# Activations stored features-first, their two parts side by side, and passes of 320, 256 and 288 columns in one product

## The chip, the cores and the metric

The kernel runs on one core of a Trainium2 chip. The metric is the device time of one execution in microseconds (us); the median of three runs is compared. TensorE (PE) does matrix products, VectorE (DVE) and ScalarE (ACT) elementwise work, GpSimd (POOL) some of it, and SyncE (SP) issues most transfers.

## What is computed

One layer of a hybrid decoder for 288 tokens (a prompt of 256 and 8 samples of 4), model width 2048, float32:

```python
h = rms_norm(x, g_pre)
z = h @ w_in                        # q | k | v | u | v_g
A = block-sparse attention over q, k, v (samples also read a paged cache of 2048 past tokens)
B = gelu(u) * (tril(w_spatial) @ layer_norm(gelu(v_g)) + b_spatial)
mix = (sigmoid(h @ wg_a) * (A @ w_a_out) + sigmoid(h @ wg_b) * (B @ w_b_out)) @ w_o
x = x + rms_norm(mix, g_post_mix)
a1, g1 = split(rms_norm(x, g_pre_ffn) @ w_ffn_in)          # 2 x 5632 columns
x = x + rms_norm((silu(a1) * g1) @ w_ffn_out, g_post_ffn)
x = x + (p @ w_ple) * sigmoid(rms_norm(x, g_ple) @ w_ple_gate)
```

It returns x (called y), the new k and v rows for the cache and the normalised v_g rows of the samples.

## The kernel before, in words

**Layout.** Every activation lies in SBUF with 128 features on the partitions and the 288 tokens (T) along the row, one such block for each of 16 feature groups k (KD = 16). In memory x, p, y and the k rows have tokens first, so the kernel turns them on TensorE with transposes of 128x128: x at the start (`turn` in `h_parts`, L147, tile `pt`), x once more for the residual while w_o runs (tile `xc`), p (tile `ptok`), the spatial weights (L469, `wt`), the k rows on their way out (`to_tokens`, L315, `tt`) and y at the end (L1045, `yt`).

**Product.** All weight products go through `product` (L236 to 260): 256 output columns of a weight at a time, as two halves t of 128, each with an accumulator of 288 float32 in a PSUM bank. Every float32 factor is split into a high and a low part of the type fp32r. A weight tile `wr` of 512 KB (four k) is loaded by SP (L245), ACT casts it to `wh` (L248), DVE subtracts to get `wl` (L249). For each k and t three passes of 288 columns follow: wh with the activation's high part (L255), wh with its low part (L256), wl with the high part (L257). A tile thus feeds 24 passes. There are 496 tiles of four k and 24 of two, which makes 4064 triples or 12,192 passes. Four buffers hold `wr`, three each `wh` and `wl`.

**Stages.** In order of time: q (tiles `hh`, `hl` from x), k, v, v_g, the gates and u with b between them while the cache is read and the sample scores and values are computed (to 699 us), a (w_a_out, to 750), o (w_o, to 857), the norm and residual, fa and fg (w_ffn_in, first half, 869 to 1151), f (w_ffn_out, first half, 1152 to 1293), fa and fg again (1300 to 1572), f again (to 1713.7), norm and residual, pg (w_ple_gate, 1726.6 to 1835), and the tail that adds up y and stores it. `le` is the small product with w_ple that is put into the two norms. f has 16 accumulators over 22 k each in two halves, so 704 triples; when one is complete, `fo_done` copies or adds it to `fo` (L1008, L1010).

**Order.** The instruction order of each engine comes from a scheduler; every engine works its queue in that order. At the start SP's queue interleaves parts of x, the weight tiles of w_in and pages of the key cache (`kt`).

Of the kernel before, what the change touches and what calls it, by code (L numbers as in the profile page):

```python
# [10 lines left out]
F32 = mybir.dt.float32  # L11
# [97 lines left out]
def tile_hybrid_step(ctx: ExitStack, tc: tile.TileContext, a: dict, o: list):  # L109
    nc = tc.nc  # L110
    y_p, y_s, kp_o, vp_o, ks_o, vs_o, gv_o = o
# [20 lines left out]

    cst = perm.tile([128, 128], F32, name="cst")
    nc.sync.dma_start(cst, a["c_perm"][:, :128])
# [7 lines left out]
    TP = 3 * 128  # L142

    def turn(pt, tiles, c):

        for j, t in enumerate(tiles):
            nc.tensor.transpose(pt[:, j * 128:j * 128 + 128], t[:, c], ident)  # L147

    xp = a["x_prompt"].rearrange("b s d -> (b s) d")
    xs = a["x_sample"].rearrange("b s d -> (b s) d")  # L150
    srcs = [(xp[0:128], 128), (xp[128:256], 128), (xs, TS)]
    XC = 512
    x_tok = [[p_x0.tile([128, XC], F32, name=f"x{j}_{c}") for j in range(3)] for c in range(D // XC)]

    def x_load(c):
        for (src, n), t in zip(srcs, x_tok[c]):
            nc.sync.dma_start(t[:n], src[:, c * XC:c * XC + XC])

    for tiles in x_tok:
        clear_rows(tiles[2])  # L160
    x_load(0)
    names = ["g_pre_mix", "g_post_mix", "g_pre_ffn", "g_post_ffn", "g_ple", "g_vnorm"]
    glist = [a[name].rearrange("l (k p) -> (l k) p", p=128) for name in names]
    gl0 = p_x0.tile([16, 128], F32, name="gl0")
    nc.scalar.dma_start(gl0, glist[0])
    gl = p_x0.tile([72, 128], F32, name="gl")
    for i, g in enumerate(glist[1:]):
        nc.gpsimd.dma_start(gl[16 * i:16 * i + g.shape[0]], g)
# [19 lines left out]
    def turned_gains(gl, n):  # L188
        gains = perm.tile([128, n], F32, name=f"gains{n}")
        gp = bank([128, n], "gp")  # L190
        nc.tensor.transpose(gp, gl, ident[:n, :n])
        nc.vector.tensor_copy(gains, gp)
        return gains

    g_pre = turned_gains(gl0, 16)

# [9 lines left out]
    hh = p_h.tile([128, KD, T], F32R, name="hh")  # L206
    hl = p_h.tile([128, KD, T], F32R, name="hl")

    def h_parts(c):
        for i in range(XC // 128):  # L210
            k = c * (XC // 128) + i
# [4 lines left out]
            nc.vector.scalar_tensor_tensor(hl[:, k], pt, g_pre[:, k:k + 1], hh[:, k], op0=ALU.mult, op1=ALU.subtract)  # L216

    def square_sums(c):
        for j in range(3):
            junk = p_x0.tile([128, XC], F32, name="junk", bufs=2)  # L220
            nc.scalar.activation(junk, x_tok[c][j], AF.Square, accum_out=sums[:, j, c:c + 1])

    sums = p_x0.tile([128, 3, D // XC], F32, name="sums")
    r0 = p_h.tile([128, T], F32, name="r0")

    def r0_of():
        st = p_x0.tile([128, 3], F32, name="st")
        nc.vector.tensor_reduce(st, sums, axis=AX.X, op=ALU.add)
        r0p = bank([128, TP], "r0p")
        for j in range(3):  # L230
            dg = p_x0.tile([128, 128], F32, name="dg", bufs=3)
            nc.vector.tensor_scalar(dg, ident, st[:, j:j + 1], None, op0=ALU.mult)
            nc.tensor.matmul(r0p[:, j * 128:j * 128 + 128], ones_d, dg, start=True, stop=True)
        rstd_of(r0, r0p[:, :T], p_x0.tile([128, T], F32, name="r0t"))


    def product(w, c0, ks, part, done, name, of="acc"):
# [26 lines left out]
    def hpart(k):  # L264
        return hh[:, k], hl[:, k]
# [9 lines left out]
    for c in range(D // XC):  # L275
        h_parts(c)
        for q in q2:
            next(q)
        if c + 1 < D // XC:
            x_load(c + 1)  # L280
        square_sums(c)
    r0_of()
    gains = turned_gains(gl, 72)
    g_pm, g_pf, g_pof, g_pl, g_vn = (gains[:, 16 * i:min(16 * i + 16, 72)] for i in range(5))
# [146 lines left out]
    def gmlp_gen():  # L431
# [26 lines left out]
        def prep_gen():  # L458
            gm = p_g.tile([128, C_GM], F32, name="gm")
            nc.sync.dma_start(gm, a["c_gm"])  # L460
            wsp = p_g.tile([128, H, 128], F32, name="wsp", tag="vn")
            nc.sync.dma_start(wsp, a["w_spatial"].rearrange("l g t s -> t (l g) s"))
            nc.sync.dma_start(brow, a["b_spatial"].rearrange("l g t -> l (g t)").to_broadcast([128, H * 128])
                              .rearrange("p (g t) -> p g t", t=128))
            tri = gm[:, C_TRI:C_TRI + 128][:, None, :].to_broadcast([128, 4, 128])
            for g in range(0, H, 4):
                tp = bank([128, 4, 128], "wt")
                for t in range(4):
                    nc.tensor.transpose(tp[:, t], wsp[:, g + t], ident)  # L469
                nc.vector.tensor_tensor(wst[:, g:g + 4], tp, tri, ALU.mult)  # L470
                yield 0.5
# [40 lines left out]
        def done_u(x, h):  # L512
            vn = late["vn"]
            for t in range(2):
# [24 lines left out]
    def gate_gen():  # L539
# [25 lines left out]
        for g in range(8):  # L565
            yield from product(w_b, g * GC, K8, lambda k: (bb[:, 0, k], bb[:, 1, k]), lambda x, g=g: done_b(x, g), "b")
# [257 lines left out]
    ah = p_ab.tile([128, H, T], F32R, name="ah")  # L824
    al = p_ab.tile([128, H, T], F32R, name="al")
# [6 lines left out]
    mh = p_m.tile([128, KD, T], F32R, name="mh")  # L832
    ml = p_m.tile([128, KD, T], F32R, name="ml")
# [3 lines left out]
    def mix_gen():  # L837
        for g in range(8):
# [8 lines left out]
            yield from product(w_a, g * GC, K8, lambda k: (ah[:, k], al[:, k]), done, "a")  # L847
# [6 lines left out]

    p_xt, end_xt = pool("p_xt", "left")
    for c in range(4):
        xc = [p_xt.tile([128, 512], F32, name=f"xc{j}", bufs=2) for j in range(3)]
        clear_rows(xc[2])
        for (src, n), t in zip(srcs, xc):
            nc.sync.dma_start(t[:n], src[:, c * 512:c * 512 + 512])  # L860
        for k in range(4):
            pt = bank([128, TP], "pt")
            turn(pt, xc, slice(k * 128, k * 128 + 128))
            nc.vector.tensor_copy(x1[:, 4 * c + k], pt[:, :T])
# [41 lines left out]
    for g in range(8):  # L906
        drain(product(w_o, g * GC, K16, lambda k: (mh[:, k], ml[:, k]), lambda x, g=g: wo_done(x, g), "o"))

    p_z, end_z = pool("p_z", "right")
    zh = p_z.tile([128, KD, T], F32R, name="zh")  # L910
    zl = p_z.tile([128, KD, T], F32R, name="zl")
# [21 lines left out]
    pp_ = a["p_prompt"].rearrange("l b s c -> (l b s) c")  # L933
    ps_ = a["p_sample"].rearrange("l b s c -> (l b s) c")
    psrc = [(pp_[0:128], 128), (pp_[128:256], 128), (ps_, TS)]
    p_tok = [p_n.tile([128, PLE], F32, name=f"ptok{j}", tag="yt", bufs=3) for j in range(3)]
    clear_rows(p_tok[2])
    for (src, n), t in zip(psrc, p_tok):
        nc.sync.dma_start(t[:n], src)
    ph = p_n.tile([128, 2, T], F32R, name="ph")  # L940
    pl = p_n.tile([128, 2, T], F32R, name="pl")
    for k in range(2):
        pt = bank([128, TP], "pt")
        turn(pt, p_tok, slice(k * 128, k * 128 + 128))
        pt = pt[:, :T]
        nc.scalar.copy(ph[:, k], pt)
        nc.vector.tensor_tensor(pl[:, k], pt, ph[:, k], ALU.subtract)
# [27 lines left out]
    def zpart(k):  # L975
        return zh[:, k], zl[:, k]
# [111 lines left out]
```

## Time and profile before

| | |
|---|---|
| median of three runs | 1848.33 us (1846.85 to 1848.41) |
| the profiled execution: its time | 1845.0 us |
| its span, first to last instruction | 1843.2 us |
| PE busy | 1822.8 us, 99% |
| DVE, ACT, POOL busy | 52%, 42%, 5% |
| mean granted TensorE clock | 0.997 |
| moved by DMA | 414.83 MB, mean 225 GB/s |

The duration of a PE row contains its way through a pipeline: passes that begin 133 ns apart show some 296 ns each. What a pass costs in a full stream is therefore read from the distance of the starts (the chain in order of time, or the count of passes in a window), not from its mean duration.

### The profile page before, as it was taken

Reading aid. Unit: us, or ns where it says so; the run is one execution under the profiler, and the core shown is the slowest. Engines: PE = TensorE matmul, PEld = TensorE weight load, DVE = VectorE, ACT = ScalarE, POOL = GpSimd, SP = SyncE. Lnnn points to the kernel's source line nnn. Section 1 sums busy time; section 2 is a strip of 40 time slices with the busy share of each in tenths; the row PEclk is TensorE's granted clock in tenths of the full one; section 3 lists DMA queues with packets and bytes.
Section 4 is the critical chain, followed back from the end, with each engine's and each line's share of the span. In section 5 each row is a group of like instructions: output and inputs, shape, how many; then the busy total and the mean of one; then the engine's idle time right before and its main releaser. Section 6 shows DMA issues by size and latency. Waiting matters only on the chain.

```text
span 1843.2 us, 38883 instructions
## 1 busy us (share of the span) xinstructions
PE 1822.8 (99%) x16004; PEld 1775.4 (96%) x16004; DVE 951.8 (52%) x1357; ACT 775.2 (42%) x1090; POOL 97.8 (5%) x195
## 2 busy tenths in 40 slices
PE   8999999999999999999999999999999999999898
PEld 8999899999999989999999999999999999999898
DVE  4754446544444347635855554433545545444764
ACT  5334455434333344445533333333333333434643
POOL 2010112000000000110000000000000000001000
PEclk9999999999999999999999999999999999999999
DMA  9589999999999985544555554445555555444452
GB/s 344 168 297 350 329 354 329 365 344 363 356 340 353 374 280 180 181 164 138 167 162 170 162 170 162 163 163 166 172 162 170 162 170 162 164 161 155 137 192 101
DMA packets 312673, 414.83 MB, mean 225 GB/s; under 512 B 13544, under 2 KB 275296, under 8 KB 312496
## 3 DMA queue, kind: packets, MB, share of 16 engines
q1 hardware_dynamic: 311120, 409.23, 64.7%
q8 instruction: 125, 2.05, 0.4%
q0 software_dynamic: 1200, 2.76, 0.4%
q10 hardware_dynamic: 176, 0.37, 0.1%
q14 instruction: 52, 0.43, 0.1%
HBM read 407.45 MB, written 4.85 MB: 224 GB/s over the span
## 4 chain that ended last, share of the span: by engine, by line
PE 97%; DVE 1%; ACT 1%; issue 0%; DMA 0%; SPq 0%; DVEq 0%
PE f L256 5%; PE f L257 5%; PE fa L257 5%; PE f L255 5%; PE fg L257 5%; PE fg L255 5%; PE fg L256 5%; PE fa L255 5%; PE fa L256 5%; PE values L732 3%; PE scores L634 3%; PE ga L255 2%; PE pg L255 2%; PE gb L255 2%; PE ga L256 2%; PE pg L257 2%
## 5 line engine op out<-in xcount | busy, mean ns | idle before, releaser
L249 DVE TENSOR_TENSOR wl<-wr,wh 128x1024 fp32r<-128x1024 f32 (+1 forms) x520 | 623.9, 1201 | 719.9 <-ACT wh L248 708.1
L248 ACT CAST wh<-wr 128x1024 fp32r<-128x1024 f32 (+1 forms) x520 | 535.8, 1031 | 896.0 <-PE f L256 165.2
L257 PE MATMUL f<-dh,wl 128*128 128x288 f32 x704 | 208.9, 297 | 0.0
L256 PE MATMUL f<-dl,wh 128*128 128x288 f32 x704 | 208.5, 296 | 0.0
L255 PE MATMUL f<-dh,wh 128*128 128x288 f32 x704 | 207.5, 295 | 0.0
L255 PE MATMUL fg<-zh,wh 128*128 128x288 f32 x704 | 207.3, 295 | 0.0
L257 PE MATMUL fg<-zh,wl 128*128 128x288 f32 x704 | 207.2, 295 | 0.0
L257 PE MATMUL fa<-zh,wl 128*128 128x288 f32 x704 | 206.7, 295 | 0.5 <-DVE wl L249 0.5
L256 PE MATMUL fa<-zl,wh 128*128 128x288 f32 x704 | 206.0, 294 | 0.9 <-DVE zl L925 0.9
L256 PE MATMUL fg<-zl,wh 128*128 128x288 f32 x704 | 206.9, 294 | 0.0
L255 PE MATMUL fa<-zh,wh 128*128 128x288 f32 x704 | 204.7, 295 | 1.0 <-ACT zh L924 1.0
L256 PEld LDWEIGHTS fa<-zl,wh 128*128 128x128 f32 x704 | 132.5, 188 | 1.2 <-DVE zl L925 1.2
L257 PEld LDWEIGHTS fa<-zh,wl 128*128 128x128 f32 x704 | 132.0, 188 | 0.7 <-DVE wl L249 0.7
L256 PEld LDWEIGHTS fg<-zl,wh 128*128 128x128 f32 x704 | 132.7, 188 | 0.1
L256 PEld LDWEIGHTS f<-dl,wh 128*128 128x128 f32 x704 | 132.6, 188 | 0.0
L255 PEld LDWEIGHTS fa<-zh,wh 128*128 128x128 f32 x704 | 131.4, 188 | 1.2 <-ACT zh L924 1.2
L255 PEld LDWEIGHTS f<-dh,wh 128*128 128x128 f32 x704 | 132.3, 188 | 0.1
L255 PEld LDWEIGHTS fg<-zh,wh 128*128 128x128 f32 x704 | 132.3, 188 | 0.0
L257 PEld LDWEIGHTS fg<-zh,wl 128*128 128x128 f32 x704 | 132.1, 188 | 0.1
L257 PEld LDWEIGHTS f<-dh,wl 128*128 128x128 f32 x704 | 132.1, 188 | 0.1
L255 PE MATMUL pg<-zh,wh 128*128 128x288 f32 x256 | 76.1, 304 | 5.4 <-ACT zh L924 5.4
L255 PE MATMUL gb<-hh,wh 128*128 128x288 f32 x256 | 76.7, 299 | 0.0
(356 smaller groups left out, 3792.2 us busy)
## 6 DMA issues: line engine op xcount, KB each, us to landing
wr<-in_w_ffn_in SPq DMA_DIRECT2D x176, 512.0 KB, 3.4
kt<-in_cache_k SPq DMA_DIRECT2D x128, 512.0 KB, 7.4
vt<-in_cache_v SPq DMA_DIRECT2D x128, 512.0 KB, 6.5
wr<-in_w_in SPq DMA_DIRECT2D x80, 512.0 KB, 6.3
wr<-in_w_ffn_out SPq DMA_DIRECT2D x80, 512.0 KB, 3.2
wr<-in_w_gate SPq DMA_DIRECT2D x64, 512.0 KB, 6.8
wr<-in_w_o SPq DMA_DIRECT2D x32, 512.0 KB, 3.2
wr<-in_w_ple_gate SPq DMA_DIRECT2D x32, 512.0 KB, 3.2
```

The costliest lines, as they stand in the source:

```text
L248: nc.scalar.copy(wh[:, :m], raw[:, :m])
L249: nc.vector.tensor_tensor(wl[:, :m], raw[:, :m], wh[:, :m], ALU.subtract)
L255: nc.tensor.matmul(accs[t], wh[:, i, c], xh, start=k == 0, stop=False)
L256: nc.tensor.matmul(accs[t], wh[:, i, c], xl, start=False, stop=False)
L257: late["mm"] = nc.tensor.matmul(accs[t], wl[:, i, c], xh, start=False, stop=k == n - 1)
L634: i = nc.tensor.matmul(sp[b][32 * g:32 * g + 32, 4 * n:4 * n + 4], Q[:, h2, g, dq], kt[:, :, c:c + 32], start=h2 == 1 and dq == 0, stop=h2 ...
L732: i = nc.tensor.matmul(oa[b][32 * g:32 * g + 8], w[:, n, 32 * g + 8 * part:32 * g + 8 * part + 8], v[:, :, g], start=first and part == 3, ...
```

## The change

The host hands over x, p, the gains and w_spatial with features on the partitions, and takes y and the k rows in that form, so all transposes of these are gone; k and y are stored straight from the tiles `kT` and `x1`. x comes in four pieces of 590 KB (`xs`), and for the residual once more in one transfer of 2.36 MB into `x1`. The mean of the squares at the start is taken from squares of `xs` (ACT, in place), DVE additions and two float32 matmuls over 288 columns, instead of row sums and three matmuls over 128. The high and low parts of an activation lie side by side in one tile (`hhl`, `ahl`, `mhl`, `phl`, `zhl`, `dhl`, `bb`), a row of 2x288. With that, `product` has a parameter `wide`: the first pass takes 288 + wide columns, so that it also does the first `wide` columns of wh times low; the second pass does the remaining 288 - wide; the third is as before. The first columns of the low part land in extra columns of the accumulator, which ACT copies out (`rest`) and DVE adds. `wide=32` is given to f alone (320, 256, 288); elsewhere it is 0.

```diff
-        accs = [bank([128, T], f"{name}{t}", of) for t in range(2)]
+        accs = [bank([128, T + wide], f"{name}{t}", of) for t in range(2)]
...
-                xh, xl = part(k)
+                x = part(k)
                 for t in range(2):
                     c = slice(t * 128, t * 128 + 128)
-                    nc.tensor.matmul(accs[t], wh[:, i, c], xh, start=k == 0, stop=False)
-                    nc.tensor.matmul(accs[t], wh[:, i, c], xl, start=False, stop=False)
-                    late["mm"] = nc.tensor.matmul(accs[t], wl[:, i, c], xh, start=False, stop=k == n - 1)
+                    nc.tensor.matmul(accs[t], wh[:, i, c], x[:, :T + wide], start=k == 0, stop=False)
+                    nc.tensor.matmul(accs[t][:, wide:T], wh[:, i, c], x[:, T + wide:], start=False, stop=False)
+                    late["mm"] = nc.tensor.matmul(accs[t][:, :T], wl[:, i, c], x[:, :T], start=False, stop=k == n - 1)
             yield 0.74 * m
-        done(accs)
+        for acc in accs if wide else []:
+            rest = perm.tile([128, wide], F32, name="rest", bufs=2)
+            nc.scalar.copy(rest, acc[:, T:])
+            nc.vector.tensor_tensor(acc[:, :wide], acc[:, :wide], rest, ALU.add)
+        done([acc[:, :T] for acc in accs])
...
-            pt = bank([128, TP], "pt")
-            turn(pt, x_tok[c], slice(i * 128, i * 128 + 128))
-            pt = pt[:, :T]
-            nc.scalar.activation(hh[:, k], pt, AF.Copy, scale=g_pre[:, k:k + 1])
+            nc.scalar.activation(hh[:, k], xs[c][:, i], AF.Copy, scale=g_pre[:, k:k + 1])
...
+        nc.scalar.activation(xs[c], xs[c], AF.Square)
+        if c:
+            nc.vector.tensor_tensor(xs[0], xs[0], xs[c], ALU.add)
...
+            nc.tensor.matmul(r0p, ones_d, q[:, i], start=i == 0, stop=i == 1)
...
-                to_tokens(kT[:, h + t], c[:, :, s], cs[:, s])
-            rows_out(kp_o, ks_o, h, c, cs)
+            nc.gpsimd.dma_start(k_o[:, h:h + 2], kT[:, h:h + 2])
...
-            nc.tensor.matmul(r0p[:, j * 128:j * 128 + 128], ones_d, dg, start=True, stop=True)
...
-                    nc.tensor.transpose(tp[:, t], wsp[:, g + t], ident)
...
-            turn(pt, xc, slice(k * 128, k * 128 + 128))
-            nc.vector.tensor_copy(x1[:, 4 * c + k], pt[:, :T])
+    nc.sync.dma_start(x1, a["x"])
...
-            drain(product(w_fo, g * GC, ks, lambda k: (dh[:, k], dl[:, k]), lambda x, g=g: fo_done(x, g), "f"))
+            drain(product(w_fo, g * GC, ks, lambda k: dhl[:, k], lambda x, g=g: fo_done(x, g), "f", wide=32))
...
-                nc.tensor.transpose(pt[:n, i * 128:i * 128 + 128], x1[:, 2 * g - 2 + i, j * 128:j * 128 + n], ident)
-            yt = p_n.tile([128, 512], F32, name="yt", bufs=3)
-            nc.scalar.copy(yt[:n], pt[:n])
-            nc.sync.dma_start(outs[j][:, (g // 2) * 512:(g // 2) * 512 + 512], yt[:n])
+        nc.sync.dma_start(y_o[:, 2 * g:2 * g + 2], x1[:, 2 * g:2 * g + 2])
```

PE's queue at the start of the program, before (`wake` is the warming up, `gp` the gains, `pt` the turned x, `q_162` and `q_163` the first accumulators):

```order
L185 MATMUL wake<-ones_d 128x128 x10
L191 MATMUL gp<-cst,gl_101 128x16
L147 MATMUL pt<-cst,x_0_78 128x128 x2
L147 MATMUL pt<-cst,x_0_79 128x128 x2
L147 MATMUL pt<-cst,x_0_80 128x128 x2
```

and in the changed kernel:

```order
L168 MATMUL wake<-ones_d 128x128 x10
L225 MATMUL q_116<-hhl,wh 128x288
L226 MATMUL q_116<-hhl,wh 128x288
L225 MATMUL q_117<-hhl,wh 128x288
L226 MATMUL q_117<-hhl,wh 128x288
```

The passes of q now follow the warming up directly.

SP's queue at the start, before (`wr` are weight tiles, `x2` behind a row means twice, `kt` a page of the key cache):

```order
L134 DMA cst<-in_c_perm 128x128
L157 DMA x_0_78<-in_x_prompt 128x512
L157 DMA x_0_79<-in_x_prompt 128x512
L157 DMA x_0_80<-in_x_sample 32x512
L245 DMA wr<-in_w_in 128x4x256 x2
```

```order
L157 DMA x_3_89<-in_x_sample 32x512
L245 DMA wr<-in_w_in 128x4x256 x4
L595 TENSOR_LOAD pt_sb
```

and in the changed kernel:

```order
L137 DMA x_76<-in_x 128x1152
L215 DMA wr<-in_w_in 128x4x256 x2
L137 DMA x_77<-in_x 128x1152
L215 DMA wr<-in_w_in 128x4x256 x2
L137 DMA x_78<-in_x 128x1152
L137 DMA x_79<-in_x 128x1152
L556 TENSOR_LOAD pt_sb
L556 ISA x2
L557 ISA
L557 DMA kt<-in_cache_k 128x1024
L215 DMA wr<-in_w_in 128x4x256
```

Before, four more tiles were ahead of the first page (eight in all); now four are, and the pages and tiles alternate behind them. In both queues the next twelve pages stand among the tiles; of these the last stands behind eleven tiles before, and behind eight in the changed kernel.

DVE's queue at the end of f, in the changed kernel (`f_20764` and `f_20765` are the last two accumulators, `rest` the extra columns, `rt_fo` the first step of the norm behind it):

```order
L219 TENSOR_TENSOR wl<-wr,wh 128x512 x3
L232 TENSOR_TENSOR f_20764<-f_20764,rest 128x32
L951 TENSOR_TENSOR fo<-fo,f_20764 128x288
L219 TENSOR_TENSOR wl<-wr,wh 128x512
L232 TENSOR_TENSOR f_20765<-f_20765,rest 128x32
L951 TENSOR_TENSOR fo<-fo,f_20765 128x288
```

The two small additions are the new rows; the others stood there before under other line numbers.

## Rows read from the trace of the kernel before

**Rows 1.** The page: busy time by engine, and the chain that ended last.
```profile
PE 1822.8 (99%) x16004; PEld 1775.4 (96%) x16004; DVE 951.8 (52%) x1357; ACT 775.2 (42%) x1090; POOL 97.8 (5%) x195
...
PE 97%; DVE 1%; ACT 1%; issue 0%; DMA 0%; SPq 0%; DVEq 0%
```

**Rows 2.** Windows: length, PE, PEld, DVE, ACT, POOL busy (count); clock; DMA share; GB/s.
```profile
20.00:45.00 25.00, 23.91 (x178) 22.87 (x177) 11.70 (x19) 11.11 (x19) 0.00 (x0) 1.00 1.03 396
...
699.00:751.00 52.00, 52.00 (x396) 52.00 (x395) 37.23 (x64) 22.77 (x33) 0.00 (x0) 1.00 0.52 172
...
900.00:1130.00 230.00, 230.00 (x1735) 229.79 (x1734) 121.53 (x157) 91.27 (x115) 0.00 (x0) 1.00 0.53 167
1160.00:1290.00 130.00, 130.00 (x977) 130.00 (x977) 50.15 (x45) 47.15 (x58) 0.00 (x0) 1.00 0.50 165
...
1713.70:1727.00 13.30, 7.94 (x55) 7.49 (x54) 10.29 (x16) 9.52 (x21) 0.00 (x0) 0.87 0.73 233
1727.00:1730.00 3.00, 3.00 (x14) 3.00 (x14) 3.00 (x7) 3.00 (x7) 0.00 (x0) 0.50 0.05 18
```

**Rows 3.** PE's waits by releaser: total, times, longest.
```profile
PE pg L255 <- ACT zh L924: 5.4, 1, 5.4
```

**Rows 4.** Transposes and similar by source line: duration min/median/max ns, first and last start.
```profile
L147 PE MATMUL pt<-cst,x x48: 270/273/474, 5.9 to 38.5; 128*128 128x128 f32 x48
L147 PE MATMUL pt<-cst,xc x48: 270/272/273, 698.9 to 775.7; 128*128 128x128 f32 x48
...
L147 PE MATMUL pt<-cst,ptok x6: 270/272/273, 857.4 to 858.0; 128*128 128x128 f32 x6
...
L315 PE MATMUL tt<-cst,kT x24: 270/273/329, 92.4 to 141.0; 128*128 128x128 f32 x16, 128*32 128x128 f32 x8
...
L469 PE MATMUL wt<-cst,wsp x8: 272/272/273, 291.2 to 291.9; 128*128 128x128 f32 x8
...
L1045 PE MATMUL yt<-cst,x x48: 270/272/329, 1765.6 to 1839.0; 128*128 128x128 f32 x32, 128*32 128x128 f32 x16
...
L233 PE MATMUL r0p<-dg,ones_d x6: 274/275/275, 44.5 to 45.1; 128*128 128x128 f32 x6
```

**Rows 5.** The chain in order of time: start us, us, what.
```profile
34.59 1.00 PE pt L147 x9
...
1717.49 0.48 PE nrm L889 x2
...
1728.42 0.24 PE pg L256
...
1730.63 0.26 PE pg L255 x2
```

**Rows 6.** Windows, the q passes alone.
```profile
0.00:49.20 49.20, 33.51 (x229) 30.97 (x229) 0.58 (x2) 1.00 0.94 338
```

**Rows 7.** SP's queue in the first 75 us: start, us, operation.
```profile
29.36 6.41 SPq L596 DMA_DIRECT2D kt<-in_cache_k  x6
36.45 36.92 SPq L245 DMA_DIRECT2D wr<-in_w_in  x12
```

**Rows 8.** DMA issues: count, KB each, median us from issue to landing.
```profile
wr<-in_w_a_out SPq DMA_DIRECT2D x16, 512.0 KB, 3.2
...
out<-yt SPq DMA_DIRECT2D x8, 256.0 KB, 2.9
```

**Rows 9.** The timeline of the tail: start, us, operation.
```profile
1836.78 0.82 DVE L1038 TENSOR_TENSOR x<-x,pgt 128x288 f32<-128x288 f32 x2
...
1838.63 1.66 SPq L1048 DMA_DIRECT2D out<-yt  x3
```

**Rows 10.** Small operations of DVE and ACT by line and form: busy, mean ns.
```profile
L757 DVE COPY A<-at 128x32 f32<-128x32 f32 x8 | 1.5, 186 | 0.4 <-PE at L756 0.3
L527 DVE TENSOR_TENSOR sp<-sp,brow 128x32 f32<-128x32 f32 x8 | 1.4, 193 | 0.0
...
L711 ACT COPY pt<-pop 128x128 f32<-128x128 f32 x8 | 2.2, 270 | 1.2 <-PE pop L709 1.2
```

More of the change, by code (lines that the diff above doesn't have):

```diff
@@ L131, in tile_hybrid_step, with x_load @@
     end_banks = banks(acc=6 - AUX, aux=AUX, long=2)
+    XK = 4
+    xs = [p_x0.tile([128, XK, T], F32, name=f"x{c}") for c in range(KD // XK)]
+    def x_load(c):
+        nc.sync.dma_start(xs[c], a["x"][:, c * XK:c * XK + XK])
+    gains = perm.tile([128, 88], F32, name="gains")
+    nc.scalar.dma_start(gains, a["gains"])
+    g_pre, g_pm, g_pf, g_pof, g_pl, g_vn = (gains[:, 16 * i:min(16 * i + 16, 88)] for i in range(6))
+    x_load(0)
     cst = perm.tile([128, 128], F32, name="cst")
-    nc.sync.dma_start(cst, a["c_perm"][:, :128])
+    nc.gpsimd.dma_start(cst, a["c_perm"][:, :128])
     ident = cst
@@ L140, in clear_rows @@
         nc.gpsimd.memset(t[64:128], 0.0)
[L142 to L168, printed above, removed]
     pt_sb = p_kv.tile([1, NB * NPG], I32, name="pt_sb")
@@ L218, in square_sums @@
[L218 to L223, printed above, removed]
+        for i in range(XK):
+            k = c * XK + i
+            nc.scalar.activation(hh[:, k], xs[c][:, i], AF.Copy, scale=g_pre[:, k:k + 1])
+            nc.vector.scalar_tensor_tensor(hl[:, k], xs[c][:, i], g_pre[:, k:k + 1], hh[:, k], op0=ALU.mult, op1=ALU.subtract)
@@ L224, in tile_hybrid_step, with squares @@
+    def squares(c):
+        nc.scalar.activation(xs[c], xs[c], AF.Square)
+        if c:
+            nc.vector.tensor_tensor(xs[0], xs[0], xs[c], ALU.add)
     r0 = p_h.tile([128, T], F32, name="r0")
     def r0_of():
[L227 to L232, printed above, removed]
-            nc.tensor.matmul(r0p[:, j * 128:j * 128 + 128], ones_d, dg, start=True, stop=True)
@@ L234, in r0_of, with product @@
-        rstd_of(r0, r0p[:, :T], p_x0.tile([128, T], F32, name="r0t"))
-    def product(w, c0, ks, part, done, name, of="acc"):
-        accs = [bank([128, T], f"{name}{t}", of) for t in range(2)]
+        q = xs[0]
+        nc.vector.tensor_tensor(q[:, 0:2], q[:, 0:2], q[:, 2:4], ALU.add)
+        r0p = bank([128, T], "r0p")
+        for i in range(2):
+            nc.tensor.matmul(r0p, ones_d, q[:, i], start=i == 0, stop=i == 1)
+        rstd_of(r0, r0p, p_x0.tile([128, T], F32, name="r0t"))
+    def product(w, c0, ks, part, done, name, of="acc", wide=0):
+        accs = [bank([128, T + wide], f"{name}{t}", of) for t in range(2)]
@@ L274, in tile_hybrid_step @@
     q2 = [q_gen(0), q_gen(1, "long")]
-    for c in range(D // XC):
+    for c in range(KD // XK):
         h_parts(c)
@@ L845, in done @@
                     nc.vector.tensor_tensor(ml[:, m], ta[:, m], mh[:, m], ALU.subtract)
[L847 removed]
+            yield from product(w_a, g * GC, K8, lambda k: ahl[:, k], done, "a")
     drain(mix_gen())
@@ L930, in residual @@
         ssq[key] = [src[:, 0], src[:, 1]]
[L933 to L947, printed above, removed]
+    p_f32 = p_n.tile([128, 2, T], F32, name="p_f32")
+    nc.sync.dma_start(p_f32, a["p"])
+    phl = p_n.tile([128, 2, 2 * T], F32R, name="phl")
+    ph, pl = phl[:, :, :T], phl[:, :, T:]
+    nc.scalar.copy(ph, p_f32)
+    nc.vector.tensor_tensor(pl, p_f32, ph, ALU.subtract)
     w_ple = a["w_ple"].rearrange("l k c -> (l k) c")
@@ L1076 @@
     c_perm, c_mix, c_gm = constants()
+    inputs = {n: np.asarray(v) for n, v in inputs.items()}
     given = {n: np.ascontiguousarray(inputs[n]) for n in _INS} | {"c_perm": c_perm, "c_mix": c_mix, "c_gm": c_gm}
+    given["x"] = features(inputs["x_prompt"], inputs["x_sample"])
+    given["p"] = features(inputs["p_prompt"], inputs["p_sample"])
+    given["gains"] = np.ascontiguousarray(np.concatenate([inputs[n].reshape(-1, 128) for n in _GAINS]).T)
+    given["w_spatial"] = np.ascontiguousarray(inputs["w_spatial"][0].transpose(2, 0, 1))
     given["cache_k"] = key_blocks(given["cache_k"])
@@ L1086 @@
     r = _run(nc, [arrays], core_ids=[0])
-    return tuple(r.results[0][f"out_{i}"] for i in range(len(_OUTS)))
+    return outputs(*(r.results[0][f"out_{i}"] for i in range(len(_OUTS))))
```

103 lines of the change are left out of this document (36 added, 67 removed).

## The prediction

> **What bounds the kernel now.** I read the page first, for the engine without idle time: PE is busy 99% of the span, and the chain that ended last is PE for 97% [rows 1]. Then the windows by stage: PE has no gap from 900 to 1130, from 1160 to 1290 and from 699 to 751, at a granted clock of 1.00 and about half of the DMA engines' time [rows 2]. So in these stages each PE instruction taken out or shortened is worth what it occupies in the stream, and work on other engines is worth nothing while PE does not wait for it. Last I looked for the places where this does not hold: the start, where DMA runs at a share of 1.03 (396 GB/s) and PE is busy 23.91 of 25 us [rows 2]; the hole of norm and residual before pg, where PE waits 5.4 us in one piece [rows 3]; and the tail.
>
> What an instruction occupies is read from distances. A transpose: nine take 1.00 us, 0.11 each [rows 5]. A pass of 288 columns: 977 begin in 130.00 us of f, 133.1 ns each, and 1735 in 230.00 us of fa and fg, 132.6 each [rows 2].
>
> **The transposes and the rows out.** The stream loses k's 24 transposes (the eight narrow ones count as full), 24 x 0.11 = 2.6 us; w_spatial's 8, 0.9; the residual's 48 (`xc`), all between 698.9 and 775.7, 5.3; and of y's 48 the 36 ahead of the last product, 4.0 [rows 4, 5]. Together -12.8 us. Nothing waits in their place: k and y are stored from tiles that exist anyway, by queues with no row among PE's long waits. p's six transposes lie in the hole before fa, whose end the residual sets, so 0 (at most -0.7) [rows 4]. The residual's x now comes in one transfer ahead of the seventh tile of w_a_out. At 172 GB/s for a share of 0.52 [rows 2], all engines move some 331 GB/s, and 2.36 MB take 7.1 us. A tile takes 3.2 us from issue to landing [rows 8] and feeds 24 passes, also 3.2 us; it is issued when the tile four ahead of it in `wr` is used up for the casts, so some 12.8 us ahead of its use, and 7.1 + 3.2 = 10.3 us fit. 0, and at most +7.1 if that cover is gone.
>
> **The start.** Until 49.2 us PE did 229 passes of q [rows 6], 30.5 us of work, the 48 transposes of x, 5.3, and six small matmuls `r0p`, 0.7 [rows 4]; the other 12.8 us are waiting and the first load. Here taking out PE work gives only what the loads allow. In the queue before, the last of the first twelve cache pages stood behind eleven weight tiles, and six cache pages were issued from 29.36 on, weight tiles alone again from 36.45 [rows 7]. Now it stands behind eight. PE can run 8 x 24 = 192 passes and then needs the ninth tile. Ahead of that lie x (2.36 MB), nine tiles and twelve cache pages (21 x 0.524 MB) and some 0.3 MB of constants, 13.7 MB. The windows give 338 GB/s over the first 49.2 us, 16.6 MB [rows 6], and 396 from 20 to 45 [rows 2]; going back from 49.2 at 396, 13.7 MB are reached at about 41.9 us. With the cast the ninth tile's passes start near 43, after which tiles land faster (1.3 us) than they are used. By 49.2 that makes 192 + 6.2/0.133 = 239 passes, ten more than before, -1.3 us; the six small matmuls ran in that time, and so do now two over 288 columns, four passes of 0.24 (the shape of `nrm` [rows 5]), 0.3 more. I take **-2**. Bounds: -7 if the loads set nothing (5.3 + 0.7 + a tile landing 1.3 earlier), +1 if the cache pages hold the ninth tile some 3 us longer.
>
> **The tail.** The last addition ends at 1836.78 + 0.82 = 1837.60; y then went through transposes, copies and the last store, issued in a group from 1838.63 [rows 9], to the end at 1843.2. Now the store follows the addition: 1837.60 + 0.4 for the issue + 2.9 to land [rows 8] = 1840.9. **-2.3.**
>
> **The extra columns in f.** 32 copies of 128x32 on ACT and additions of 128x32 on DVE. No PSUM copy of that size is on ACT in the trace; DVE's takes 186 ns, ACT's of 128x128 270 [rows 10], so 0.19 to 0.27; the addition 193 ns. DVE and ACT are busy 50 and 47 of 130 us in f [rows 2], so all but the last pair are hidden; that pair stands at the head of the chain into the hole. **+0.6** (two additions, one copy), and without cover 32 x 0.45 = +14, which would need PE to wait for accumulators; it has two pairs in hand.
>
> **The three passes of f.** Columns per triple stay 864; only their division changes: 320 + 256 + 288. What matters is how a pass's time goes with its columns, and all fp32r passes in the trace have 288. Three rows bear on it. With the clock at 0.50, the 1.2 GHz level, after the idle time before pg, a pass takes 0.24 us, exactly 288 columns at 1.2 GHz; as the clock comes back it is 0.13 [rows 5], where 288 columns at 2.4 GHz would be 120.0 ns. So the array takes one column a cycle and 13 ns are added at the full clock alone. A float32 pass over the same 288 columns takes 0.24 (`nrm`, [rows 5]), two cycles a column, with nothing added. The 13 ns can be a fixed piece per pass (then the sum of three does not change), a feeding rate below one column a cycle (proportional, no change either), or a rounding to steps of 64 columns: 288 to 320, which at 2.4 GHz is 133.3 ns. Under the last, 320 costs what 288 does and 256 costs 106.7 to 110 (a transpose, 256 cycles, shows 0.11): -23.1 to -26.6 ns per triple, x 704 = -16.3 to -18.7 us. Against strict rounding speaks that no pass could then be below 133.3: 1735 need 231.3 us, but began in 230.00; and 977 need 130.3, in 130.00 [rows 2]. And in the cold stretch nothing is rounded. The other bound: a pass cannot go below 133 while 320 pays its 32 columns, 13.3 ns x 704 = +9.4. I take **0**, nearest to a plain line through what the rows show.
>
> The Trainium skill, TensorE: Matmul & The Clock Gate, section "Back-to-back issue gap", gives an isolated pass as columns over 1.2 GHz when cold and columns over 2.4 GHz plus 2.5 ns when warm. The cold row agrees (0.24 us); the warm one does not (122.5 ns by the Trainium skill, 132.6 to 133.1 here). By it f's triple would cost 367.5 ns both before and after, so f's term would be 0 as well; the measured pass, read as a rounding, would make it -17.5. The measured rows decide, and they leave the form open.
>
> **The sum**, against the profiled execution's 1845.0: -12.8 (stream) - 2 (start) - 2.3 (tail) + 0.6 (rest) + 0 (f) = -16.5, so 1828.5. That execution lies 3.3 us below the median of the runs, 1848.33; the same difference on the median gives **1831.8 us**.
>
> **Rivals.**
> - *Passes go in steps of 64 columns.* For it: f's 133.1 ns lies within 0.2 of the 133.3 that 320 columns take; against it the two counts above. f falls by 16 to 19: 1831.8 - 17.5 = 1814, with the start's bounds 1809 to 1817.
> - *The loads take it back.* The ninth tile comes later than I work out (+1 instead of -2), or x's one transfer holds w_a_out's seventh tile (up to +7.1). For it: DMA at 1.03 of its time at the start; against it: a share of 0.52 in a. 1835 to 1842.
> - *No pass below 133 ns.* Something other than columns (the weights' path) sets the distance; 256 is not cheaper and 320 pays. Against it: transposes with their own weights pass in 110. 1831.8 + 9.4 = 1841.
> - *Other side: the place of the operands sets a pass's distance.* Every product now reads its two parts from one tile at other addresses. The trace shows 132.6 in one stage and 133.1 in another with the same shapes, so a place can be worth 0.5 ns. There are 12,192 passes; from 16.5 / 12,192 = 1.35 ns a pass it eats the whole gain, and at 2.5 ns the kernel takes 1831.8 + 30.5 = 1862. Against it: the spread seen is less than half the turning point.
>
> **Numbers.** Chances: forecast 0.48 (its own range 1827 to 1836), steps of 64 columns 0.32, loads 0.08, floor 0.07, place of operands 0.05.  The range 1810 to 1840 takes in the forecast, nearly all of the steps' case and half of the loads'. A measurement here tells about 0.2%, 3.7 us, from no change; faster means below 1844.6: 0.93, same 0.03 and slower 0.04 (loads at their worst together with the floor, or the operands' place).
>
> **What would show it.** In the changed trace: no `pt`, `tt`, `wt` or `yt` rows; the a and o stages together 5 us shorter, k 2.6, pg 3.9; the first passes of q stalled before the ninth tile near 34 to 43 us; the last store landing some 3 us behind the last addition. In f, the distances behind a pass of 320 and of 256 columns decide the largest open term: sums near 400 ns a triple are the forecast, near 375 the steps, near 412 the floor. Wrong would be the forecast if passes outside f change their distance by over 1 ns, or if a wait for `wr` appears in a.

## The result and the profile after

The changed kernel takes 1830.24 us (median of four runs, 1829.19 to 1830.55), the kernel before 1847.67 in the same comparison: a ratio of 0.9905, interval 0.9888 to 0.9922. Forecast were 1831.8 us, between 1810 and 1840. The profiled execution took 1830.38 us with a span of 1828.6, 14.6 us less than the span before. Of all executions in this document one is left out of its ratio: one of `before_pages12` (experiment 3) that took 6323.3 us, where the nine others took 1844.9 to 1849.3.

The medians lie 17.4 us apart, the two profiled executions 14.6. The traces show one thing that differs from one execution to the next: the granted clock. That of the kernel before was 1.00 from 6.5 to 1723.4 us. In the trace of `before_pages12`, which does the same work on PE, it was 0.50 from 10.0 to 16.8 and from 873.6 to 877.0, and the span is 1847.4. Against that trace the differences below for the start and for fa to f would be 2.6 and 1.5 us larger.

The page of the changed kernel, busy time, against [rows 1]:

```profile
PE 1801.1 (98%) x15818; PEld 1755.9 (96%) x15818; DVE 951.3 (52%) x1361; ACT 769.2 (42%) x1081; POOL 89.7 (5%) x169
```

PE has 186 rows fewer: 102 + 24 + 8 + 48 transposes, two for the gains and two of six small matmuls are 186, so the change did what it says. But PE's share fell to 98%. Its waits, by releaser (total, times, longest), say where:

```profile
PE q L225 <- ACT wh L218: 6.2, 3, 3.4
PE pg L225 <- ACT zhl L875: 5.8, 1, 5.8
PE fa L225 <- ACT zhl L875: 5.4, 1, 5.4
PE q L227 <- DVE wl L219: 2.5, 3, 1.6
```

Before, pg's 5.4 us was the only long one [rows 3]. Those of q and fa are new; of q's 6.2 us, 3.4 lie ahead of its first pass. The windows of the changed kernel, columns as in [rows 2]:

```profile
20.00:45.00 25.00, 19.71 (x135) 18.18 (x134) 19.17 (x30) 9.47 (x10) 0.00 (x0) 0.97 1.00 361
43.30:50.00 6.70, 5.29 (x22) 5.29 (x23) 4.29 (x5) 1.77 (x3) 0.00 (x0) 0.50 0.61 180
...
862.60:866.00 3.40, 3.40 (x14) 3.40 (x15) 3.40 (x8) 3.40 (x8) 0.00 (x0) 0.51 0.25 85
882.60:1132.60 250.00, 250.00 (x1885) 249.79 (x1884) 134.02 (x172) 98.64 (x124) 0.00 (x0) 1.00 0.55 169
1150.00:1280.00 130.00, 130.00 (x988) 130.00 (x987) 52.18 (x59) 49.59 (x73) 0.00 (x0) 1.00 0.52 167
```

The reader is to see three things. From 20 to 45 us PE does 135 rows where it did 178 [rows 2]; 131 of these are passes of q, and 149 were before, beside 24 transposes and five small matmuls. The DMA engines are just as full. Behind that wait, and behind the one ahead of fa, the granted clock is 0.50, the 1.2 GHz level: 22 and 14 passes begin where 50 and 26 would. And f does 988 passes in 130 us, where it did 977.

The stages' ends, each taken from the last pass that begins in it, show where the 14.6 us came from:

| stage | before, us | after, us | difference | forecast |
|---|---|---|---|---|
| start, q and k (to k's last pass) | 132.6 | 132.2 | -0.4 | -4.6 |
| v to ga | 566.2 | 563.6 | -2.6 | -0.9 |
| a and o | 158.5 | 153.8 | -4.7 | -5.3 |
| first hole (o's last pass to fa's first) | 11.7 | 13.0 | +1.3 | 0 |
| fa, fg, f, both halves | 844.7 | 841.7 | -3.0 | 0 |
| second hole | 13.0 | 13.4 | +0.4 | +0.6 |
| pg | 108.5 | 105.0 | -3.5 | -4.0 |
| tail | 8.1 | 5.9 | -2.2 | -2.3 |

That the total was right to 2 us is in part luck: a gain that did not come at the start and a longer first hole were met by two gains that were not forecast, in v to ga and in f.

The tail, from the timeline of the changed kernel:

```profile
1824.36 0.82 DVE L976 TENSOR_TENSOR x<-x,pgt 128x288 f32<-128x288 f32 x2
1825.20 0.36 SPq L977 DMA_DIRECT2D out<-x  x1
```

The store is issued as the last addition ends (1825.18) and the span ends 3.4 us later; before, transposes, copies and three stores lay there [rows 9].

### The profile page after: what moved, and what is told of

Read it like the earlier page. It is cut to its first block, busy times and chain, and to the rows that moved or that the text cites. A ratio compares the mean times of both kernels' runs of the same rounds, so it can differ in the third digit from the quotient of the medians.

```text
span 1828.6 us, 38398 instructions
## 1 busy us (share of the span) xinstructions
PE 1801.1 (98%) x15818; PEld 1755.9 (96%) x15818; DVE 951.3 (52%) x1361; ACT 769.2 (42%) x1081; POOL 89.7 (5%) x169
## 4 chain that ended last, share of the span: by engine, by line
PE 95%; DMA 2%; DVE 1%; ACT 1%; issue 0%; SPq 0%; DVEq 0%; ACTq 0%
PE f L225 6%; PE fa L225 5%; PE fg L225 5%; PE fa L226 5%; PE fa L227 5%; PE fg L226 5%; PE fg L227 5%; PE f L227 5%; PE f L226 5%; PE values L693 3%; PE scores L595 3%; PE pg L225 2%; PE gb L225 2%; PE ga L225 2%; PE pg L226 2%; PE pg L227 2%
## 5 line engine op out<-in xcount | busy, mean ns | idle before, releaser
L225 PE MATMUL f<-dhl,wh 128*128 128x320 f32 x704 | 217.1, 308 | 0.0
L225 PE MATMUL fa<-zhl,wh 128*128 128x288 f32 x704 | 207.9, 297 | 5.4 <-ACT zhl L875 5.4
L226 PE MATMUL fa<-zhl,wh 128*128 128x288 f32 x704 | 208.5, 297 | 0.0
L226 PE MATMUL fg<-zhl,wh 128*128 128x288 f32 x704 | 208.2, 296 | 0.0
L225 PE MATMUL fg<-zhl,wh 128*128 128x288 f32 x704 | 208.0, 296 | 0.0
L227 PE MATMUL fa<-zhl,wl 128*128 128x288 f32 x704 | 207.1, 295 | 0.0
L227 PE MATMUL fg<-zhl,wl 128*128 128x288 f32 x704 | 207.0, 295 | 0.0
L227 PE MATMUL f<-dhl,wl 128*128 128x288 f32 x704 | 207.0, 294 | 0.0
L226 PE MATMUL f<-dhl,wh 128*128 128x256 f32 x704 | 196.9, 280 | 0.0
L225 PEld LDWEIGHTS fa<-zhl,wh 128*128 128x128 f32 x704 | 132.7, 189 | 5.6 <-ACT zhl L875 5.6
L227 PEld LDWEIGHTS fa<-zhl,wl 128*128 128x128 f32 x704 | 133.6, 190 | 0.1
L227 PEld LDWEIGHTS fg<-zhl,wl 128*128 128x128 f32 x704 | 133.2, 190 | 0.0
L226 PEld LDWEIGHTS fa<-zhl,wh 128*128 128x128 f32 x704 | 132.8, 189 | 0.0
L226 PEld LDWEIGHTS f<-dhl,wh 128*128 128x128 f32 x704 | 132.5, 188 | 0.1
L225 PEld LDWEIGHTS fg<-zhl,wh 128*128 128x128 f32 x704 | 132.4, 188 | 0.1
L226 PEld LDWEIGHTS fg<-zhl,wh 128*128 128x128 f32 x704 | 132.3, 188 | 0.1
L227 PEld LDWEIGHTS f<-dhl,wl 128*128 128x128 f32 x704 | 132.2, 188 | 0.1
L225 PEld LDWEIGHTS f<-dhl,wh 128*128 128x128 f32 x704 | 132.0, 188 | 0.0
L225 PE MATMUL pg<-zhl,wh 128*128 128x288 f32 x256 | 75.7, 303 | 5.8 <-ACT zhl L875 5.8
L225 PE MATMUL gb<-hhl,wh 128*128 128x288 f32 x256 | 76.7, 300 | 0.0
```

Source lines behind the costliest of these rows:

```text
L225: nc.tensor.matmul(accs[t], wh[:, i, c], x[:, :T + wide], start=k == 0, stop=False)
L226: nc.tensor.matmul(accs[t][:, wide:T], wh[:, i, c], x[:, T + wide:], start=False, stop=False)
L227: late["mm"] = nc.tensor.matmul(accs[t][:, :T], wl[:, i, c], x[:, :T], start=False, stop=k == n - 1)
```

## The experiments

Two theories stood against each other in each of four questions; all kernels are edits of the changed one unless said otherwise.

**1. What the division of f's passes is worth.** `f288` takes it out, `wideall` gives it to every product, `f512` drives it to the end.

```diff
-            drain(product(w_fo, g * GC, ks, lambda k: dhl[:, k], lambda x, g=g: fo_done(x, g), "f", wide=32))
+            drain(product(w_fo, g * GC, ks, lambda k: dhl[:, k], lambda x, g=g: fo_done(x, g), "f"))
```

> The changed kernel with 288 columns in all three passes of f (no extra accumulator columns, no copy and addition behind them). Theory A, a pass costs a straight line in its columns and the new division is worth only a few ns a triple: f's two stages grow from 139.1 us to between 139.7 and 141 us each, the whole kernel by 0 to 3 us, no difference that can be told. Rival B, steps of 64 columns: 320 and 256 saved 17 us, so the kernel comes out near 1847 us. Rival C, a floor of 133 ns: 288 is cheaper and the kernel some 9 us faster.

Measured: 1831.15 us (1830.60 to 1831.30), ratio to before 0.991 (0.9893 to 0.9926): not told apart from the changed kernel. f's first half takes 139.5 us, from its first to its last pass, against 139.1 with the division and 140.7 before. Steps of 64 columns and the floor of 133 ns are both refuted. Without `rest`, the activations of q to ga, o and f also lie 256 bytes lower; o, which has no other change, kept its distance of 132.3 ns.

```diff
-            drain(product(w_fo, g * GC, ks, lambda k: dhl[:, k], lambda x, g=g: fo_done(x, g), "f", wide=32))
+            drain(product(w_fo, g * GC, ks, lambda k: dhl[:, k], lambda x, g=g: fo_done(x, g), "f", wide=224))
```

> The changed kernel with 512, 64 and 288 columns in f's passes. Theory A (straight line through 256, 288 and 320: 0.45 ns a column): 512 take 232 ns, 64 take 32, the triple stays near 396 ns and the kernel within 3 us. Rival: a pass has a floor set by its weights, which transposes passed at 110 ns or less: 64 columns take 60 to 110 ns, the triple 420 to 475 ns, and the kernel is 18 to 55 us slower.

Measured: 1884.76 us in one run. The chain by line over the same 100 us of f, first of the changed kernel and then of `f512` (share of the window for the pass of L225, L226 and L227):

```profile
by line: PE f L225 36.9%; PE f L227 33.5%; PE f L226 29.7%
```

```profile
by line: PE f L225 48.6%; PE f L227 45.2%; PE f L226 6.6%
```

The first window holds 761 passes, 253.7 triples, so the passes of 320, 256 and 288 columns take about 145, 117 and 132 ns: some 0.45 ns a column, a straight line in this stage. In the second, 636 pieces are 212 triples: 512 columns take 229 ns, as the line says (146 + 192 x 0.45 = 232), 64 take 31, but the 288 behind them 213 instead of 131. If the 288 columns still cost their 131, the time of the pass that is too short appears in the next row: 31 + 213 - 131 = 113 ns for the short one. So read, there is a floor near 110 ns and not at 133, and 256 columns just clear it. The 110 of a transpose does not bear this out, since at `nrm`'s 0.24 us for 288 float32 columns its 128 take 0.107 by their number alone. The rival won here (the triple takes 472 ns, the kernel 54.5 us more), and the line holds only above the floor; that the weights set it was not tested by itself. The Trainium skill, TensorE: Matmul & The Clock Gate, section "Back-to-back issue gap", says that in a stream the spacing is set by the weight load and the pass together, and gives 81 ns for 128 columns; no run here has an fp32r pass of 128 columns.

```diff
-    def product(w, c0, ks, part, done, name, of="acc", wide=0):
+    def product(w, c0, ks, part, done, name, of="acc", wide=32):
```

> The changed kernel with 320, 256 and 288 columns in every weight product, not in f alone. Theory A (straight line): the 3360 other triples change by at most the 2 ns by which f's triples lie below three passes of 132.6, so -7 to 0 us, with up to 1 us back at the ends of stages for the copies and additions. Rival B (the division itself took f's triples from 400 to 396 ns): -4.5 ns a triple, -15 us, near 1815 us.

Measured: 1820.89 us (1818.44 to 1822.12), 0.9851 (0.9834 to 0.9867): 9.4 us faster than the changed kernel, more than theory A allowed and less than rival B. Neither explains it. The same 250 us of fa and fg, in `wideall`:

```profile
880.70:1130.70 250.00, 250.00 (x1906) 249.79 (x1905) 140.77 (x216) 105.14 (x166) 0.00 (x0) 1.00 0.55 170
```

1906 passes against 1885, so 393.5 ns a triple against 397.9; in f the same division took 396.7 (`f288`, by the distances of starts) to 395.6. The division is worth 1 ns a triple in f, 2 in q to ga and 4 in fa and fg. The chain by line over 200 us of fa and fg in `wideall` shows where:

```profile
by line: PE fg L225 19.0%; PE fa L225 18.8%; PE fg L227 16.4%; PE fa L227 16.2%; PE fg L226 15.0%; PE fa L226 14.8%
```

For 509 triples that is 148.5, 117.1 and 128.1 ns for 320, 256 and 288 columns. The third pass, whose shape did not change, takes 4 ns less than in a triple of three equal passes, and 288 columns cost less than the middle of the other two. The line that fits f does not fit here; why is not shown.

**2. What place has to do with it.** `pad32` moves the left side of SBUF.

```diff
+    perm.tile([128, 8], F32, name="pad")
     xs = [p_x0.tile([128, XK, T], F32, name=f"x{c}") for c in range(KD // XK)]
```

> The changed kernel with 32 bytes of unused space ahead of everything on the left side of SBUF: weights and the activations of q to ga, o and f move by 32 bytes, those of b, a, fa, fg and pg stay. If the place of operands sets the 132.3 or 133.3 ns between passes, the distances of several stages change by about 1 ns in one direction or the other (4 us over the kernel for all of q to ga). If only the inner order of a tile (parts side by side or apart) sets them, nothing moves by more than 0.2 ns.

Measured: 1827.02 us (1826.55 to 1829.47), 0.9893 (0.9876 to 0.9909), an interval that overlaps the changed kernel's. fa and fg, whose weights moved by 32 bytes against their activations, came closer together (pg by 0.5 ns too; q to ga, o and f, where both moved, stayed):

```profile
882.50:1132.50 250.00, 250.00 (x1895) 249.79 (x1894) 134.83 (x174) 99.88 (x126) 0.00 (x0) 1.00 0.55 170
```

131.9 ns a pass instead of 132.6. So place may count, by the relation of weights and activations rather than by either alone, and by under 1 ns a pass; one trace does not show it. Against it: fa and fg came out at 132.2 in `pages8` and `pages12_fill`, where no operand moved, b and a had weights moved against theirs as well and stayed at 133.3, and `best_pad32` below has f at the same addresses as `pad32` and another distance.

**3. What took the start's gain.** `pages12` puts the first cache page behind the twelfth weight tile, `pages8` behind the eighth (`tiles[7]`), `before_pages12` does the first in the kernel before.

```diff
+            if not issued:
+                st.enter_context(tc.issue_after(tiles[11].ins))
             if len(issued) >= 4:
                 st.enter_context(tc.issue_after(issued[-4].ins))
```

> The changed kernel with the first cache page put behind the twelfth weight tile in SyncE's queue. Theory A, the start is lost to the ninth weight tile that stands behind twelve cache pages, and to the lower clock after that wait: no wait of TensorE over 1 us between 15 and 60 us, clock 1.00 from 20 to 70, q's last pass at 63 to 66 us instead of 72.0, and the kernel 5 to 8 us faster. Rival: the cache stage has no DMA time to spare, so the later pages come back as waits of the score products before 130 us, and the kernel gains under 2 us.

Measured: 1821.52 us (1820.33 to 1822.66), 0.9856 (0.984 to 0.9873), 8.7 us faster than the changed kernel, a little more than theory A said. The window from 20 to 45 us, of `pages12`:

```profile
20.00:45.00 25.00, 25.00 (x186) 24.79 (x186) 18.22 (x26) 10.02 (x11) 0.00 (x0) 1.00 0.86 290
```

182 passes of q and four small matmuls, no gap, full clock; q's last pass begins at 63.4 us instead of 72.0, k's at 123.6 instead of 132.2. Nothing comes back later: v and ga end 8.5 us earlier too.

> The changed kernel with the first cache page behind the eighth weight tile, where it stood in the kernel before. Theory A, the change's start is lost to the place of the cache pages alone (fourth tile instead of eighth): the wait for the ninth tile is gone or under 1 us, q's last pass comes at 63 to 65 us, and the kernel is 7 to 9 us faster than the changed one, as pages12 was. Rival: with TensorE ahead of the loads any twelve cache pages among the tiles hold it, and half of the wait stays: 3 to 5 us faster.

Measured: 1823.40 us (1821.90 to 1824.19), 0.9871 (0.9855 to 0.9887), 6.8 us faster than the changed kernel. q's last pass begins at 66.2 and k's at 126.4, so the place of the pages is worth 5.7 of the 8.5 us that `pages12` gained up to there. The wait for the ninth tile is gone. One of 1.5 us for the tenth tile's low part is left, and it is not for a load: the tile landed at 37.1, and its low part stands in DVE's queue behind the first norm's steps (39.0 to 40.8). Theory A is right on the cause and too high on the size; part of the 6.8 us comes later, from fa and fg at 132.2 ns a pass instead of 132.6.

> The kernel before with its first cache page behind the twelfth weight tile. Theory A: the change's work taken out of the start (48 transposes of 0.11 us and their waits) was hidden by the loads; without these the kernel before gains less than the 8.7 us of the changed kernel, 3 to 5 us, since its transposes now are in the way: about 1844 us, and the change is worth 21 to 24 us between the two. Rival: both gain the same 8 to 9 us (1839.5), and the work taken out is worth nothing at the start whatever the loads do.

Measured: 1848.71 us against 1848.71 for the kernel before, 0.9998 (0.9988 to 1.0008): nothing. Both expectations missed. The window shows why:

```profile
20.00:45.00 25.00, 23.91 (x178) 22.87 (x177) 11.58 (x20) 11.87 (x24) 0.00 (x0) 1.00 0.55 176
```

PE's busy time and count are those of [rows 2], 23.91 and 178, although the DMA engines' share fell from 1.03 to 0.55. That both agree to the digit is chance (151 passes and 27 transposes here; 149, 24 and five small matmuls there), but the loads did not hold PE in either: in the kernel before, the ninth, tenth and eleventh tile landed at 29.3, 33.1 and 35.7 us and were cast at 34.5, 43.1 and 44.6. PE's own work, with the transposes and their short gaps, filled the window. In this trace q's last pass begins at 72.8 us instead of 70.2, with the clock at 0.50 from 10.0 to 16.8; the medians are the same.

**4. What the lower clock costs.** `pages12_fill` is `pages12` with matmuls of ones behind le in both holes.

```diff
+    def fill(n):
+        with tc.issue_after(late["mm"].ins):
+            ps = bank([128, 128], "fill")
+            for _ in range(n):
+                nc.tensor.matmul(ps, ones_d, ones_d, start=True, stop=True)
...
     le_products(range(LE))
+    fill(22)
...
     le_products(range(LE, 8))
+    fill(22)
```

> As pages12, and 22 matmuls of ones (128x128, float32, into an accumulator that nobody reads) behind the last pass of le in both norm and residual holes, so that TensorE is not idle there. Theory A, the one idle piece of 5.7 and 6.1 us lets the clock fall to 1.2 GHz for 3.4 us behind it, which costs some 1.5 us each: the granted clock stays at 1.00 behind both holes, and the kernel is 2 to 3.5 us faster than pages12 (1821.5 us). Rival: the holes are set by the chain on DVE and ACT alone and the clock costs nothing on the path: no change, or up to 1 us slower where the ones hold the first pass.

Measured: 1817.69 us (1816.92 to 1818.34), 0.9834 (0.9818 to 0.9851), 3.8 us faster than `pages12`. The first 8 us of fa and of pg, in `pages12` and then in `pages12_fill` (in `pages12` the clock is 0.50 until 860.3 and until 1713.6):

```profile
854.10:862.10 8.00, 7.97 (x39) 7.97 (x40) 8.00 (x15) 3.86 (x8) 0.00 (x0) 0.61 0.13 45
1710.40:1718.40 8.00, 7.95 (x49) 7.95 (x50) 8.00 (x16) 5.15 (x11) 0.00 (x0) 0.80 0.02 6
```

```profile
855.00:863.00 8.00, 8.00 (x60) 8.00 (x61) 8.00 (x15) 4.59 (x9) 0.00 (x0) 1.00 0.09 28
1707.50:1715.50 8.00, 8.00 (x60) 8.00 (x61) 7.96 (x15) 4.59 (x9) 0.00 (x0) 1.00 0.02 8
```

21 and 11 passes more at 0.133 us are 2.8 and 1.5 us; the holes themselves keep their 13.0 and 13.4 us. Theory A holds, with a gain a little above its range. Besides, fa's and fg's distances came out at 132.2 instead of 132.6 ns at the same addresses, some 1.1 us over the rest of both halves, and fa's first pass came 0.9 us later, at 855.0; together 4.5, against 4.4 us between the two spans.

**5. Together.** `all_three` is `pages12_fill` with `wide=32` everywhere.

> As pages12_fill, with 320, 256 and 288 columns in every weight product. If the three gains are separate they add up: 1821.5 (pages12) - 9.3 (wideall against the changed kernel) - 3 = 1809 us, between 1806 and 1813. If the gain of wideall came from the start or the holes in part, it is less: 1813 to 1818.

Measured: 1812.54 us (1811.54 to 1813.66), 0.9807 (0.9791 to 0.9824). At the end of what was expected: the gains add up, less 3.5 us. Its waits show part of the rest: `pg` now waits 1.5 us and `fa` 1.0 for DVE's low part, since a pass of 320 columns needs the low part's first 32 at once.

In `best` the products at a stage's edge take 288 columns again; three of the edits:

```diff
-        drain(product(w_o, g * GC, K16, lambda k: mhl[:, k], lambda x, g=g: wo_done(x, g), "o"))
+        drain(product(w_o, g * GC, K16, lambda k: mhl[:, k], lambda x, g=g: wo_done(x, g), "o", wide=32 * (g < 7)))
...
-            drain(product(w_ple, g * GC, [0, 1], lambda k: phl[:, k], lambda x, g=g: le_done(x, g), "le"))
+            drain(product(w_ple, g * GC, [0, 1], lambda k: phl[:, k], lambda x, g=g: le_done(x, g), "le", wide=0))
...
-    pg = [product(w_pg, g * GC, K16, zpart, lambda x, g=g: pg_done(x, g), "pg") for g in range(8)]
+    pg = [product(w_pg, g * GC, K16, zpart, lambda x, g=g: pg_done(x, g), "pg", wide=32 * (2 < g < 7)) for g in range(8)]
```

> all_three without the extra columns where a stage ends or begins on the path: le, the first products of q, fa, fg and pg, and the last ones of ga, o, f and pg take 288 columns; all others 320, 256, 288. If the waits of 0.5 to 1 us that all_three showed there came from the extra copies and additions and from the low parts that a pass of 320 needs at once, it is 1 to 3 us faster than all_three (1812.5): 1810 to 1811.5. Rival: the waits move elsewhere: no difference.

Measured: 1809.53 us (1808.23 to 1812.02), 0.9799 (0.9783 to 0.9815): 3.0 us faster than `all_three`, 20.7 faster than the changed kernel and 38 faster than the one before, the fastest measured.

> best with the 32 unused bytes of pad32 ahead. If the distance of passes hangs on the place of the weights against the activations, fa, fg and pg move by 1 to 2 ns a triple (1 to 3 us over the kernel, either way); q to ga, o and f stay. If pad32's gain came with the 288-column passes alone, nothing moves.

Measured: 1813.21 us (1812.64 to 1813.88), 0.9813 (0.9797 to 0.983), 3.7 us slower than `best`. It did not go as either said: fa, fg and pg stayed, and f, o, a and b became slower by 1.1 to 1.5 ns a pass. 100 us of f, in `pad32` and then in `best_pad32`:

```profile
1160.00:1260.00 100.00, 100.00 (x761) 100.00 (x760) 41.01 (x47) 39.85 (x59) 0.00 (x0) 1.00 0.52 169
```

```profile
1160.00:1260.00 100.00, 100.00 (x752) 100.00 (x751) 40.14 (x47) 39.45 (x58) 0.00 (x0) 1.00 0.51 165
```

The same product, division and addresses, and 131.8 against 133.3 ns a pass (759 and 750 begin in the window; the column also counts two that began ahead of it).

## Why the prediction was right, and which of its steps were not

**The transposes in the stream: right.** a and o lost 4.7 us of the 5.3 forecast. Against the forecast stand a new wait of a for ga's last values (0.4), two `nrm` matmuls that moved out of the hole into o (0.5) and the new distances of a's and o's passes (+0.3 and -0.8). pg lost 3.5 of 4.0; its first 4.9 us ran at a clock of 0.50, where it was 3.7 us before, which is 0.6. x's one transfer took 11.8 us to land instead of 7.1, and no wait for a tile of w_a_out appeared: the cover held.

**The tail and the last pair of the extra columns: right**, -2.2 for -2.3 and +0.4 for +0.6; `f288`, without the extra columns, has the second hole back at 13.0 us.

**f's division: right in size, incomplete in reason.** The term was 0. f's two stages lost 1.6 us each (140.7 to 139.1), and `f288` keeps 1.2 of that without the division (139.5), so the division itself gave 0.8 us in both. The line through the columns is what the prediction took; the rounding, its strongest rival at 0.32, is refuted by 145, 117 and 132 ns. Of the two counts that it set against the rounding, one was misread: the 977 of f [rows 2] take in two passes that began before the window, and the 975 that begin in it lie 133.3 ns apart, just what the rounding asks. That of fa and fg holds, 1733 in 230.00 us, 132.7 each, and was the one to trust.

**The start: the step that failed.** The prediction read a DMA share of 1.03 beside 12.8 us without PE work as "taking out PE work gives only what the loads allow". Some 9 of these 12.8 us lie ahead of the first pass (9.4 us into the span), and the times of landing and cast under `before_pages12` show that in the kernel before the loads held nothing between 20 and 45 us. PE's own work was the bound there; taking it out was worth 8.9 us in start, q and k together, as `pages12` shows (123.6 against 132.6 for k's last pass); the transposes of x and k, 5.3 + 2.6, and 0.7 from the 768 passes that lie 0.9 ns closer (below) account for 8.6 of it. The two traces differ in clock, though: `pages12` began 17 passes up to 13.8 us, at half speed, where 34 would begin at full clock. Without these 2.2 us the gain is near 11; of the rest, `pt`'s waits of 1.5 and 1.2 us for DVE and for x are gone too.

But the order in SP's queue, first cache page behind the fourth weight tile, made the loads the bound in the changed kernel and took it back. The estimate for the ninth tile's landing, 41.9 us, was good: it landed at 41.2, and the wait ends at 42.3, when its cast is done. What the sum left out comes behind it: the cast's low part stands in DVE's queue behind the rotation of q's first product (`rope`), 1.9 us more until 44.7, and then the clock is at 0.50 until 50, 22 passes instead of some 50 in 6.7 us. Forecast -4.6 with k's transposes, measured -0.4 (-3.0 against the trace of `before_pages12`, whose first passes ran at the lower clock too).

**The first hole: two mechanisms were not foreseen.** p's six transposes were costed at nothing because the residual sets the hole's end. It does, but that end came 1.3 us later. In DVE's queue two low parts of the next stage's weight tiles now stand among the four steps of the norm that the residual needs (L174 to L177); from the changed kernel's timeline:

```profile
856.64 1.22 DVE L219 TENSOR_TENSOR wl<-wr,wh 128x1024 fp32r<-128x1024 f32 x1
857.78 0.30 DVE L176 TENSOR_SCALAR rt_mo<-rt_mo 128x288 f32<-128x288 f32 x1
858.24 1.23 DVE L219 TENSOR_TENSOR wl<-wr,wh 128x1024 fp32r<-128x1024 f32 x1
859.38 0.45 DVE L177 TENSOR_TENSOR r_mo<-r_mo,rt_mo 128x288 f32<-128x288 f32 x1
```

The norm's last step begins 9.8 us behind o's last pass; before, with the four steps in a row, it was 6.8. This is read from the rows; no run puts the two back. The second mechanism is the clock. The transposes had kept le's passes apart and later; now le runs right behind o, PE is idle for 5.4 us in one piece, the clock falls, and fa's first 3.4 us run at half speed, 14 passes instead of 26, or 1.6 us. In `pages12` it was 6.2 us, and `pages12_fill` shows 2.8 us for it. The kernel before was not free of it: in the trace of `before_pages12` the clock fell behind its hole as well, for 3.4 us.

**The distances of passes: seen as the place of operands, with the other sign.** The rival was priced as a loss from 1.35 ns a pass. What came was a gain of 0.9 ns a pass in q to ga and in o (133.4 to 132.5 on average), and a loss of 1.0 in b and a. Over 4224 and 768 passes that is -3.8 and +0.8 us: most of v to ga's -2.6, and in f a gain of 1.1 ns gave the 2.4 us that `f288` keeps. That the operands' new places did this is not shown: no run moves them alone back. The prediction had the 0.5 ns between stages in view and gave them no term.

**Open.** What sets a stage's distance within 131 to 133.4 ns is not settled. Addresses may move it (`pad32`, and four stages of `best_pad32`), but `pages8`, `pages12_fill` and `best_pad32` show other distances at the same addresses, so the state in which the stream enters a stage seems to count too; that was not tested by itself.

## What to carry to other kernels

When work is taken off the engine that is busy, look at what the queues ahead of it do next: here 8.7 us hung on whether loads that nobody needed for 60 us stood ahead of the ninth weight tile, and, by the rows, 1.3 us on two operations that slipped in among the steps of a norm. A full DMA queue beside a busy engine is no proof that it binds; compare when a tile lands with when it is used, or take the traffic away and see if the engine's rows change. Work that fills a hole may cost nothing and still be worth something: it keeps the clock up, and 22 matmuls of ones in each of two holes gave more than the columns of f did.

## What the runs showed of the hardware

- fp32r passes at the full clock cost some 0.45 ns a column in f (117, 132 and 145 ns for 256, 288 and 320 columns), with no steps of 64; in fa and fg of `wideall` the same three took 117, 128 and 148.5. In `f512`, a pass of 64 columns and the 288 behind it took 31 + 213 ns, which puts the short one near 113.
- Passes of 288 columns in an unbroken stream began 131.9 to 133.3 ns apart on average, depending on stage and kernel; fa's came out at 131.9 with 32 bytes of padding, and at 132.2 to 132.6 without.
- An idle piece of PE of 5.4 us was followed by a granted clock of 0.50 in every trace that has it, for 3.4 us of the changed kernel's fa and 6.2 of `pages12`'s; 22 small matmuls in the hole kept it at 1.00. In the changed kernel's start, in the second of two gaps of 2.8 and 1.9 us between passes, the clock fell to 0.50 for 6.8 us; behind one gap of 1.8 us (`pages8`) it stayed at 1.00.
